# Tokens on partitions for the residual stream, and a Strassen down projection, in a two-layer decoder trunk

## The chip, the cores and the metric

One core of one Trainium2 chip. The metric is the device time of one execution in microseconds (us). Three runs of the kernel before gave 1452.82, 1452.92 and 1454.23; the median is 1452.92.

## The reference

Two pre-norm layers over 512 tokens of width 1024, all in float32:

```
for i in 0, 1:
    h = rms_norm(x, norm_mix[i])
    x = x + mixer_i(h)                      # 0: gated delta rule + differential attention; 1: forgetting attention
    h = rms_norm(x, norm_mlp[i])
    x = x + square(relu(h @ w_mlp_up[i])) @ w_mlp_down[i]          # 1024 -> 4096 -> 1024
    x = x + (p[i] @ w_ple_proj[i]) * sigmoid(x @ w_ple_gate[i])    # 256 -> 1024, 1024 -> 1024
out = rms_norm(x, norm_final)
```

Each mixer ends with a projection of its eight heads' outputs, `y = heads @ w_out` (1024 by 1024).

## The kernel before, in words

**Products.** Every large product is made exact to about float32 by splitting both operands in a high part (rounded to the fast format, by ScalarE) and a low part (the difference, by VectorE), and taking three matmuls a k tile of 128: high by high, low by high, high by low. A weight arrives by DMA on SyncE's queue in pieces of 512 KB (`wraw`, into one of three buffers `raw`), and `wsplit` makes the pair of it (one of three buffers `whl`, 8 KB a partition). `wload` does that for two pieces, 1024 rows by 256 columns. `gemm` makes one tile of 128 features by 512 tokens in 24 matmuls of 512 columns: the weight is the stationary operand, the activations move.

**The residual stream** lies with features on partitions: `x_all`, eight tiles of 128 features by 512 tokens. In layer 0 it is read anew in `out_proj`, 256 columns at a time, and turned by 32 transposes of 128 by 128. `norm_tile` weights and splits a feature tile at once; the factor of each token (`norm_sum`, `norm_spread`: eight matmuls of 2 columns and two of 512) is applied later, behind the next product. That is what lets the next product start before the norm's sum is known. `p_proj` (the product of the layer's input embedding) stands between `out_proj` and the MLP, and `norm_sum` is put in its middle. In layer 1 the first query and key projection of the mixer (`ahead`) plays that part.

**MLP.** The 4096 hidden features go in four groups g of 1024. `up_group(g)` makes eight tiles u (24 matmuls each; relu and factor on VectorE, the square on GpSimd, the split on ScalarE and VectorE). `down_group(g)` makes eight tiles of 24 matmuls and adds each to the stream (`add_x`). The order is up 0, up 1, down 0, up 2, down 1, up 3, down 2, down 3. A layer has 768 matmuls up and 768 down.

**Order of the work.** The program's text gives priorities; a scheduler at compile time orders each engine's instructions by them and by which operands its own timing of the program has ready. So a later product's matmuls can stand between the steps of an earlier chain on TensorE. Every engine runs its own list in order, waiting at semaphores; so does each queue that issues DMAs (SyncE's for weights, ScalarE's for small inputs).

**Rooms.** Tiles come from pools. The pools `cp`, `raw`, `whl` and `hl` (16 tiles of 4 KB, for the split activations) live through the whole program. The mixers' pools (`gp` in layer 0, `fp` in layer 1) are closed when the mixer's text ends, and the pools opened after that (`xp`, `lp`, `tp`, then `mp`, `qp`) take the same room. `p_split` loads p into `pr`, a tile of `tp`, by a DMA on ScalarE's queue.

**The last part** (`ple_last`) turns the stream to tokens on partitions by 32 transposes, and makes 16 tiles of 128 tokens by 256 features, 24 matmuls of 256 columns each.

Of the kernel before, what the change touches and what calls it, by code (L numbers as in the profile page):

```python
# [10 lines left out]
F32 = mybir.dt.float32  # L11
# [31 lines left out]
def constants():  # L43
    """Masks, the identity and the rotary frequencies: they depend on shapes alone."""
# [23 lines left out]
MM = 3  # banks of the projections' sums  # L68
LAT_A, LAT_B = 1.55, 1.7  # stretch the waits between the steps of a chain of delta rule, of attention
W_G, W_B, W_T, W_V, W_Q = 10.0, 22.5, 20.0, 6.0, 3.6  # waits for what a chain starts from  # L70
Z_B, DSTEP = 3, 3.47
ORDER = "a0 a1 w0 v0 v1 b0 b1 a2 a3 w2 b2 b3"
ABREAST = 2  # heads of the delta rule at once
N_SP = 10  # tiles of theirs
N_ST = 5  # short-lived ones
N_WARM = 15  # products that bring TensorE's clock up


class Tensor:
    """TensorE, and how much work it has been given (us)."""  # L80
# [4 lines left out]
    def matmul(self, out, lhsT, rhs, start, stop):  # L85
        self.time += math.prod(rhs.shape[1:]) * (1 if rhs.dtype == F32R else 4) / 2400
        return self.tc.nc.tensor.matmul(out, lhsT=lhsT, rhs=rhs, start=start, stop=stop)  # L87
# [7 lines left out]
def trunk(ctx: ExitStack, tc: tile.TileContext, I, cst, out):  # L95
# [43 lines left out]
    # ------------------------------------------------------------------ constants  # L139
# [12 lines left out]
    xT, shared = [], {}  # L152
    cols = cp.tile([P, R_ALL], F32, name="cols")
    rstd_c = cp.tile([P, NT], F32, name="rstd_c")
# [58 lines left out]
    def narrow_steps(ws, act, pool, tag, bufs):  # L213
        """Eight columns of a projection, tokens on partitions; ws has high and low parts side by side."""
# [17 lines left out]
    def rsqrt(dst, ss, w, scale, eps=EPS, big=None, V=V):  # L232
        """dst = (ss * scale + eps) ** -0.5; with big, 0 where the sum has left the range."""
# [11 lines left out]
    def norm_tile(k, nrm, wcol):  # L245
        """One feature tile of x: its weighted split, and its share of the mean square."""
        hi, lo = hl()
        w = cols[:, wcol + k:wcol + k + 1]
        S.activation(out=hi, in_=xT[k], func=AF.Copy, scale=w)  # L249
        V.scalar_tensor_tensor(out=lo, in0=xT[k], scalar=w, in1=hi.bitcast(F32), op0=ALU.mult, op1=ALU.subtract)  # L250
        nrm["act"].append((hi, lo))
        if k == 0:
            S.activation(out=nrm["s"], in_=xT[k], func=AF.Square)
        else:
            q = nrm["pool"].tile([P, T], F32, tag="sq", name="sq", bufs=2)
            S.activation(out=q, in_=xT[k], func=AF.Square)  # L256
            G.tensor_tensor(out=nrm["s"], in0=nrm["s"], in1=q, op=ALU.add)  # L257

    def norm_begin(pool):
        s = pool.tile([P, T], F32, tag="nrm_s", name="nrm_s", bufs=1)  # L260
        return {"s": s, "act": [], "pool": pool}

    def norm_sum(nrm):
        parts = [nrm["pool"].tile([P, T], F32R, tag="sq", name=n, bufs=2) for n in ("s_hi", "s_lo")]
        split(*parts, nrm["s"])
        ps = aux()
        for i in range(NT):
            for j, a in enumerate(parts):
                PE.matmul(ps[:, 2 * i:2 * i + 2], lhsT=a[:, i * P:(i + 1) * P], rhs=ones_r[:, 0:2], start=j == 0,
                          stop=j == 1)  # L270
        rsqrt(rstd_c, ps[:, 0:2 * NT].rearrange("p (i c) -> p i c", c=2)[:, :, 0], NT, 1.0 / D, big=BIG)
        r = [nrm["pool"].tile([P, NT], F32R, tag=f"r{j}", name="r", bufs=1) for j in range(2)]
        split(*r, rstd_c)
        nrm["diag"] = parts
        for t, a in zip(parts, r):
            V.tensor_tensor(out=v3(t), in0=mid(ident), in1=a.bitcast(F32).broadcast_to([P, NT, P]), op=ALU.mult)

    def norm_spread(nrm):
        pb = aux()
        for j, t in enumerate(nrm["diag"]):  # L280
            PE.matmul(pb, lhsT=ones_r, rhs=t, start=j == 0, stop=j == 1)
        S.activation(out=shared["rstd_b"], in_=pb, func=AF.Copy)
        return nrm["act"]

    def add_x(m, ps):
        V.tensor_tensor(out=xT[m], in0=ps, in1=xT[m], op=ALU.add)  # L286

    # ------------------------------------------------------------------ mixer of layer 0
    def even_mixer(act, first, wba):
        w_in = I["w_in_even"][0]  # L290
        with ExitStack() as es:
# [16 lines left out]
            # gates of the delta rule: b and a columns, tokens on partitions  # L308
# [8 lines left out]
            def gates():  # L317
# [32 lines left out]
                # decays within the blocks on the diagonal  # L350
# [13 lines left out]
            def conv_tile(ps, j, name):  # L364
                """causal convolution and silu of one tile of qkv_a"""
# [1033 lines left out]
```

## Time and profile before

| | |
|---|---|
| median of three runs | 1452.92 us (1452.82 to 1454.23) |
| span of the profiled execution | 1453.0 us; the page gives no other time of it, so its own time is taken as 1453.0 |
| TensorE busy | 1420.3 us, 98%, 7095 matmuls |
| VectorE, ScalarE, GpSimd busy | 793.7 us (55%), 622.7 us (43%), 195.4 us (13%) |
| DMA | 129.46 MB, mean 89 GB/s |
| granted clock of TensorE, mean | 0.990 |

The page counts a matmul as busy from its start to a modelled end, and matmuls overlap, so the cost of one is read from start to start of the next, in the timeline. Times in rows are us from the span's start. The stages, read from TensorE's timeline: mixer of layer 0 to about 315, its output projection to 356, `p_proj` to 368, the MLP and the gate product to 773, the mixer of layer 1 to 997, its output projection to 1034, `p_proj` to 1046, the MLP to 1396, the rest to 1453.

### The profile page before, as it was taken

Reading aid. Unit: us, or ns where it says so; the run is one execution under the profiler, and the core shown is the slowest. Engines: PE = TensorE matmul, PEld = TensorE weight load, DVE = VectorE, ACT = ScalarE, POOL = GpSimd, SP = SyncE. Lnnn points to the kernel's source line nnn. Section 1 sums busy time; section 2 is a strip of 40 time slices with the busy share of each in tenths; the row PEclk is TensorE's granted clock in tenths of the full one; section 3 lists DMA queues with packets and bytes.
Section 4 is the critical chain, followed back from the end, with each engine's and each line's share of the span. In section 5 each row is a group of like instructions: output and inputs, shape, how many; then the busy total and the mean of one; then the engine's idle time right before and its main releaser. Section 6 shows DMA issues by size and latency. Waiting matters only on the chain.

```text
span 1453.0 us, 18378 instructions
## 1 busy us (share of the span) xinstructions
PE 1420.3 (98%) x7095; PEld 1184.1 (81%) x7095; DVE 793.7 (55%) x1396; ACT 622.7 (43%) x1061; POOL 195.4 (13%) x243
## 2 busy tenths in 40 slices
PE   8989988999999999999999999999999999999997
PEld 6877776778888888888888888887888888888897
DVE  6836785754454353443466856756455445354445
ACT  6746775665332231222355544545433222132244
POOL 1350056012121020100022000001122001010000
PEclk9999997999999999999999999999999999999999
DMA  6251212124233233223235443642323323323321
GB/s 175 79 102 45 59 46 59 44 73 145 88 96 107 88 98 105 88 95 108 87 88 99 64 85 73 66 89 88 94 87 101 102 88 101 101 88 102 102 98 63
DMA packets 144555, 129.46 MB, mean 89 GB/s; under 512 B 8578, under 2 KB 141524, under 8 KB 144212
## 3 DMA queue, kind: packets, MB, share of 16 engines
q1 hardware_dynamic: 140080, 123.82, 31.3%
q10 hardware_dynamic: 4388, 4.47, 1.4%
q8 instruction: 56, 0.92, 0.3%
q14 instruction: 31, 0.25, 0.1%
HBM read 126.04 MB, written 2.23 MB: 88 GB/s over the span
## 4 chain that ended last, share of the span: by engine, by line
PE 89%; DVE 3%; POOL 3%; DMA 2%; ACT 2%; issue 1%; ACTq 0%; SPq 0%; POOLq 0%; DVEq 0%
PE mm L87 78%; PE ax L87 8%; PE ax L91 2%; DMA raw<-w_in_even 1%; POOL xc L415 1%; DMA lb<-lsc 1%; POOL xt L413 1%; POOL b L389 0%; DVE whl L133 0%; DMA xr<-x 0%; POOL x L502 0%; POOL ro L615 0%; DMA pr<-p 0%; ACT L377 0%; POOL rot L673 0%
## 5 line engine op out<-in xcount | busy, mean ns | idle before, releaser
L87 PE MATMUL mm<-hl,whl 128*128 128x512 f32 x4032 | 961.8, 394 | 2.2 <-DVE whl L133 1.4
L87 PEld LDWEIGHTS mm<-hl,whl 128*128 128x128 f32 x4032 | 752.6, 189 | 157.3 <-DVE whl L133 2.1
L133 DVE TENSOR_TENSOR whl<-raw,whl 128x1024 fp32r<-128x1024 f32 (+1 forms) x223 | 295.0, 1323 | 192.7 <-ACT whl L130 192.5
L130 ACT ACTIVATE whl<-raw 128x1024 fp32r<-128x1024 f32 (+1 forms) x224 | 237.3, 1060 | 338.0 <-PE mm L87 320.1
L87 PE MATMUL mm<-ul,whl 128*128 128x512 f32 x768 | 176.5, 391 | 0.0
L87 PEld LDWEIGHTS mm<-ul,whl 128*128 128x128 f32 x768 | 144.2, 188 | 31.6
L1134 POOL TENSOR_TENSOR u<-r 128x512 f32<-128x512 f32 x64 | 66.7, 1042 | 464.5 <-DVE r L1132 464.5
L286 DVE TENSOR_TENSOR x_all<-mm,x_all 128x512 f32<-128x512 f32 x80 | 55.2, 691 | 111.6 <-PE mm L87 109.4
L87 PE MATMUL mm<-whl,hl 128*128 128x256 f32 x864 | 107.4, 284 | 0.0
L87 PEld LDWEIGHTS mm<-whl,hl 128*128 128x128 f32 x864 | 105.1, 192 | 0.3
L1132 DVE SCALAR_TENSOR_TENSOR r<-mm,rstd_b 128x512 f32<-128x512 f32 x64 | 44.3, 692 | 81.5 <-PE mm L87 74.0
L257 POOL TENSOR_TENSOR nrm_s<-nrm_s,sq 128x512 f32<-128x512 f32 x21 | 29.7, 1412 | 409.4 <-ACT sq L256 409.4
L130 ACT ACTIVATE ul<-u 128x512 fp32r<-128x512 f32 x32 | 20.2, 632 | 93.6 <-POOL u L1134 93.6
L130 ACT ACTIVATE hl<-u 128x512 fp32r<-128x512 f32 x32 | 20.2, 633 | 87.7 <-POOL u L1134 87.7
L133 DVE TENSOR_TENSOR hl<-u,hl 128x512 fp32r<-128x512 f32 x32 | 21.9, 685 | 30.1 <-ACT hl L130 30.1
L133 DVE TENSOR_TENSOR ul<-u,ul 128x512 fp32r<-128x512 f32 x32 | 21.9, 685 | 30.1 <-ACT ul L130 30.1
L844 DVE TENSOR_TENSOR ax<-ax,cmask 128x128 f32<-128x128 f32 x64 | 18.7, 295 | 17.0 <-PE ax L87 16.6
L249 ACT ACTIVATE hl<-x_all,cols 128x512 fp32r<-128x512 f32 x24 | 17.3, 721 | 24.6 <-DVE x_all L286 17.9
L130 ACT ACTIVATE hl<-x_all 128x512 fp32r<-128x512 f32 x16 | 10.0, 625 | 40.2 <-DVE x_all L286 37.9
L250 DVE SCALAR_TENSOR_TENSOR hl<-x_all,cols,hl 128x512 fp32r<-128x512 f32 x24 | 18.0, 749 | 10.6 <-ACT hl L249 10.5
L669 ACT ACTIVATE rot<-mm 32x512 f32<-32x512 f32 x32 | 18.9, 589 | 9.6 <-DMA raw<-w_in_even 4.9
L87 PE MATMUL ax<-qk 128*128 128x256 f32 (+2 forms) x96 | 21.9, 335 | 0.1
(351 smaller groups left out, 1261.4 us busy)
## 6 DMA issues: line engine op xcount, KB each, us to landing
raw<-w_mlp_up SPq DMA_DIRECT2D x64, 512.0 KB, 3.7
raw<-w_mlp_down SPq DMA_DIRECT2D x64, 512.0 KB, 3.4
raw<-w_in_even SPq DMA_DIRECT2D x32, 256.0 KB, 3.5
raw<-w_ple_gate SPq DMA_DIRECT2D x16, 512.0 KB, 3.4
raw<-w_in_odd SPq DMA_DIRECT2D x32, 256.0 KB, 6.0
raw<-w_in_odd SPq DMA_DIRECT2D x16, 512.0 KB, 4.8
raw<-w_in_even SPq DMA_DIRECT2D x12, 512.0 KB, 3.8
raw<-w_out_even SPq DMA_DIRECT2D x8, 512.0 KB, 3.4
```

The lines of the kernel that those rows point to most:

```text
L87: return self.tc.nc.tensor.matmul(out, lhsT=lhsT, rhs=rhs, start=start, stop=stop)
L91: return self.tc.nc.tensor.transpose(out, in_, ident)
L130: S.activation(out=hi, in_=src, func=AF.Copy)
L133: return (E or V).tensor_tensor(out=lo, in0=src, in1=hi.bitcast(F32), op=ALU.subtract)
L249: S.activation(out=hi, in_=xT[k], func=AF.Copy, scale=w)
L250: V.scalar_tensor_tensor(out=lo, in0=xT[k], scalar=w, in1=hi.bitcast(F32), op0=ALU.mult, op1=ALU.subtract)
L257: G.tensor_tensor(out=nrm["s"], in0=nrm["s"], in1=q, op=ALU.add)
L286: V.tensor_tensor(out=xT[m], in0=ps, in1=xT[m], op=ALU.add)
L669: S.activation(out=rot[32 * b:32 * b + 32], in_=ps[32 * (b ^ 1):32 * (b ^ 1) + 32], func=AF.Copy)
L844: V.tensor_tensor(out=ps[:, c], in0=ps[:, c], in1=cmask, op=ALU.add)
L1132: V.scalar_tensor_tensor(out=r, in0=ps, scalar=0.0, in1=rstd_b, op0=ALU.max, op1=ALU.mult)
L1134: G.tensor_tensor(out=u, in0=r, in1=r, op=ALU.mult)
```

## The change

The stream lies with tokens on partitions, `x_tok`, four tiles of 128 tokens by 1024 features, loaded by four DMAs of 512 KB on SyncE's queue after the first mixer. All products that add to it now have the activations stationary (128 tokens) and 512 columns of weights moving. The norm is applied before the next product: `Norm.scaled` makes the scaled tile of 128 tokens and `features` turns it with eight transposes and splits it. That is done in both `out_proj`, behind both MLPs, and behind the first gate product. `p_split` and `p_proj` move behind the MLP. The first four pieces of an output projection's weight go to tiles `owhl` of a pool `op` that is opened after the mixer; of the other four, three go to `whl`.

The down projection of each group is done as seven products of half-size blocks (256 tokens, 512 of k, 512 features) in Strassen's scheme in Winograd's form, 24 matmuls of 512 columns each: 168 a group in place of 192. The sums of blocks are made by GpSimd, in float32, before the split: four sums of weight blocks (two instructions of 128 by 1024 each) and four of activation blocks (two of 128 by 512 each). The squares stay on GpSimd, the relu goes to ScalarE. For the first three groups each product is followed by one tile of the next up group.

The diff, cut to its core:

```diff
+SRAW, SWHL, SA = 8, 3, 4
+ORDER_MID, ORDER_END = (1, 5, 6, 7, 3, 4, 2), (1, 2, 5, 6, 3, 7, 4)
...
-    def norm_tile(k, nrm, wcol): ...
-    def norm_begin(pool): ...
-    def norm_sum(nrm): ...
-    def norm_spread(nrm): ...
+    def tok_steps(ps, act, w, i, cs, kts, first, last):
+        for j, kt in enumerate(kts):
+            ah, al = (a[:, i * P:(i + 1) * P] for a in act[kt])
+            PE.matmul(ps, lhsT=ah, rhs=w[:, 0, j, cs], start=first and j == 0, stop=False)
+            PE.matmul(ps, lhsT=ah, rhs=w[:, 1, j, cs], start=False, stop=False)
+            PE.matmul(ps, lhsT=al, rhs=w[:, 0, j, cs], start=False, stop=last and j == 1)
+
+    def features(i, src, act):
+        for c in range(2):
+            ps = aux2()
+            for b in range(4):
+                PE.transpose(ps[:, b * P:(b + 1) * P], src[:, (4 * c + b) * P:(4 * c + b + 1) * P], ident)
+            for b in range(4):
+                hi, lo = (a[:, i * P:(i + 1) * P] for a in act[4 * c + b])
+                split(hi, lo, ps[:, b * P:(b + 1) * P])
...
+        def scaled(self, i, src):
+            t, r, ok = small(1, "tn"), small(1, "rn"), small(1, "okn")
+            V.tensor_scalar(out=t, in0=self.ssq[:, i, 0:1], scalar1=self.ssq[:, i, 1:2], scalar2=EPS, ...)
+            V.tensor_scalar(out=ok, in0=t, scalar1=BIG / D, scalar2=None, op0=ALU.is_lt)
+            V.tensor_scalar(out=t, in0=t, scalar1=BIG / D, scalar2=None, op0=ALU.min)
+            G.tensor_tensor(out=r, in0=t, in1=nhalf[:, 0:1], op=ALU.pow)
+            V.tensor_tensor(out=r, in0=r, in1=ok, op=ALU.mult)
+            xn = ...
+            V.scalar_tensor_tensor(out=xn, in0=src, scalar=r, in1=self.wb, op0=ALU.mult, op1=ALU.mult)
+            return xn
...
+    def whole_weight(w, pool, pairs=range(4)):
+        op_bufs["owhl"] = 4
+        return [[wide(w, 2 * P * j, 512 * c, rawp, *((whp,) if c and n < 3 else (pool, "raw", "owhl")))
+                 for n, j in enumerate(pairs)] for c in range(2)]
+
+    def out_proj(w, heads, norm, pairs):
+        act = [hl() for _ in range(KT)]
+        with tc.tile_pool(name="op", bufs=1) as op:
+            first, second = whole_weight(w, op, pairs)
+            sums = [acc(), acc(), acc(), aux2()]
+            for n, j in enumerate(pairs):
+                for i in range(NT):
+                    tok_steps(sums[i], heads, first[n], i, slice(0, 512), (2 * j, 2 * j + 1), n == 0, n == 3)
+            for i in range(NT):
+                add_x(i, slice(0, 512), sums[i])
+                norm.squares(i, 0, x_tok[i][:, 0:512])
+            turned = []
+            for i in range(NT):
+                ps = acc()
+                for n, j in enumerate(pairs):
+                    tok_steps(ps, heads, second[n], i, slice(0, 512), (2 * j, 2 * j + 1), n == 0, n == 3)
+                add_x(i, slice(512, 1024), ps)
+                norm.squares(i, 1, x_tok[i][:, 512:1024])
+                turned.append(norm.scaled(i, x_tok[i]))
+                if i:
+                    features(i - 1, turned[i - 1], act)
+        return act, lambda: features(NT - 1, turned[NT - 1], act)
...
+    def down_products(w, g, us, mp, order):
...
+        def combine(out, a, b, op):
+            for o, p, q in zip(out, a, b):
+                G.tensor_tensor(out=o, in0=p, in1=q, op=op)
+            return out
+        def right(p):
...
+            if p == 5:
+                sums["T"] = combine(block(0, 0), block(0, 1), block(0, 0), ALU.subtract)
+            elif p == 6:
+                combine(sums["T"], block(1, 1), sums["T"], ALU.subtract)
+            elif p == 7:
+                return combine(block(0, 1), block(1, 1), block(0, 1), ALU.subtract)
+            elif p == 4:
+                combine(sums["T"], block(1, 0), sums["T"], ALU.subtract)
+            return sums["T"]
+        def left(p):
...
+        for p in order:
+            ws = [wide_split(t, mp, "swhl") for t in right(p)]
+            acts = []
+            for t in left(p):
+                a = mp.tile([P, 2, 2, 256], F32R, tag="sa", name="sa", bufs=SA)
+                split(a[:, 0], a[:, 1], t)
+                acts.append(a)
...
+            for j in range(2):
+                for t in range(2):
...
+            for t in range(2):
+                add_x(2 * th + t, slice(512 * fh, 512 * fh + 512), banks[name][t])
+            yield p
...
             for g in range(1, 4):
-                cur = up_group(g)
-                down_group(g - 1, prev)
+                cur = []
+                ups = up_steps(g, cur)
+                for _ in down_products(down, g - 1, prev, mp, ORDER_MID):
+                    next(ups)
+                for _ in ups:
+                    pass
                 prev = cur
-            down_group(3, prev)
+            xs = [hl() for _ in range(KT)]
+            for p in down_products(down, 3, prev, mp, ORDER_END):
+                if p == 7:
+                    for i in range(2):
+                        features(i, x_tok[i], xs)
+                    between()
+            for i in range(2, NT):
+                features(i, x_tok[i], xs)
...
+        pT = []
+        xs = mlp(layer, act, last_tile, lambda: pT.extend(p_split(layer)))
+        with tc.tile_pool(name=f"qp{layer}", bufs=1) as pool:
+            pj = [pool.tile([P, D], F32, name=f"pj{i}") for i in range(NT)]
+            p_proj(layer, pT, pj)
...
+            act = ple(layer, xs, pj, pool, norm)
```

In the first up tiles of a layer the two tiles are made in halves of 256 tokens, and the last token tile's `features` (`last_tile`) stands between the halves. The gate product of layer 1 has tiles of 512, 256 and 256 columns in place of four of 256.

## Rows read from the trace of the kernel before

**Rows 1.** The page, busy time of each engine over the span.
```profile
PE 1420.3 (98%) x7095; PEld 1184.1 (81%) x7095; DVE 793.7 (55%) x1396; ACT 622.7 (43%) x1061; POOL 195.4 (13%) x243
```

**Rows 2.** The page, chain that ended last, share of the span by engine.
```profile
PE 89%; DVE 3%; POOL 3%; DMA 2%; ACT 2%; issue 1%; ACTq 0%; SPq 0%; POOLq 0%; DVEq 0%
```

**Rows 3.** Timeline of TensorE, MLP: start us, us, engine, line, operation out<-moving,stationary, form, count.
```profile
586.56 87.25 PE L87 MATMUL mm<-hl,whl 128*128 128x512 f32 x384
673.65 44.13 PE L87 MATMUL mm<-ul,whl 128*128 128x512 f32 x192
```

**Rows 4.** The same view, embedding product of layer 1: weights move, activations stand.
```profile
1041.77 4.45 PE L87 MATMUL mm<-whl,pT 128*128 128x512 f32 x18
1046.06 5.63 PE L87 MATMUL mm<-hl,whl 128*128 128x512 f32 x24
```

**Rows 5.** The same view: four transposes and what follows; the norm's small matmuls, first and last.
```profile
337.84 0.60 PE L91 MATMUL ax<-gen,raw 128*128 128x128 f32 x4
338.20 5.75 PE L87 MATMUL mm<-hl,whl 128*128 128x512 f32 x24
...
362.97 0.17 PE L87 MATMUL ax<-ones,s_hi 128*128 128x2 f32 x1
...
363.78 4.38 PE L87 MATMUL mm<-pT,whl 128*128 128x512 f32 x18
```

**Rows 6.** The same view, last gate product, 256 columns.
```profile
1403.75 41.83 PE L87 MATMUL mm<-whl,hl 128*128 128x256 f32 x346
```

**Rows 7.** The same view, layer 0: output projection's matmuls between the last heads' steps, first and resumption.
```profile
299.59 2.34 PE L87 MATMUL mm<-hl,whl 128*128 128x512 f32 x9
...
315.10 3.93 PE L87 MATMUL mm<-hl,whl 128*128 128x512 f32 x16 [0.42 <-ACT hl L916]
```

**Rows 8.** The same in layer 1, first and the one behind the last head's matmuls.
```profile
980.98 1.10 PE L87 MATMUL mm<-hl,whl 128*128 128x512 f32 x4
...
996.93 6.05 PE L87 MATMUL mm<-hl,whl 128*128 128x512 f32 x25
```

**Rows 9.** Timeline of VectorE and ScalarE's queue where the mixers end, layer 0 and layer 1.
```profile
313.73 1.47 DVE L133 TENSOR_TENSOR hl<-zt,hl 128x512 fp32r<-128x512 f32 x2
315.23 0.40 ACTq L1167 DMA_DIRECT2D pr<-p  x1
...
998.53 0.69 DVE L133 TENSOR_TENSOR hl<-gate,hl 128x512 fp32r<-128x512 f32 x1 [0.70 <-ACT hl L130]
999.31 0.39 ACTq L1167 DMA_DIRECT2D pr<-p  x1
```

**Rows 10.** Windows: stretch, length, busy PE PEld DVE ACT POOL, granted clock, DMA share, GB/s.
```profile
108.00:112.00 4.00, 2.75 (x6) 1.79 (x7) 2.68 (x7) 3.23 (x6) 0.60 (x1) 0.66 0.47 133
112.00:116.00 4.00, 4.00 (x11) 2.79 (x9) 1.35 (x4) 1.75 (x3) 0.69 (x1) 0.50 0.02 6
```

**Rows 11.** Weight tile in the MLP of layer 0 (ns min/median/max, first and last start); one collision.
```profile
L130 ACT ACTIVATE whl<-raw x64: 1046/1062/1062, 377.1 to 717.9; 128x1024 fp32r<-128x1024 f32 x64
L133 DVE TENSOR_TENSOR whl<-raw,whl x64: 1224/1226/1866, 378.2 to 719.0; 128x1024 fp32r<-128x1024 f32 x64
...
423.95 1.04 POOL L1134 TENSOR_TENSOR u<-r 128x512 f32<-128x512 f32 x1 [4.40 <-DVE r L1132]
...
424.21 1.87 DVE L133 TENSOR_TENSOR whl<-raw,whl 128x1024 fp32r<-128x1024 f32 x1 [0.40 <-ACT whl L130]
```

**Rows 12.** Instructions by line and form: busy us, mean ns; the first from one tile's view.
```profile
L257 POOL TENSOR_TENSOR nrm_s<-nrm_s,sq x21: 1275/1292/1795, 326.4 to 1036.6; 128x512 f32<-128x512 f32 x21
...
L133 POOL TENSOR_TENSOR whl<-raw,whl 128x1024 fp32r<-128x1024 f32 x1 | 2.4, 2402 | 4.3 <-ACT whl L130 4.3
L242 POOL TENSOR_TENSOR rs_t<-rs_t,nhalf 128x4 f32<-128x4 f32 x7 | 7.1, 1012 | 60.7 <-DVE rs_t L241 60.7
L286 DVE TENSOR_TENSOR x_all<-mm,x_all 128x512 f32<-128x512 f32 x80 | 55.2, 691 | 111.6 <-PE mm L87 109.4 <-ACT x_all L1112 2.1
L133 DVE TENSOR_TENSOR ul<-u,ul 128x512 fp32r<-128x512 f32 x32 | 21.9, 685 | 30.1 <-ACT ul L130 30.1
```

More of the change, by code (lines that the diff above doesn't have):

```diff
@@ L259, in norm_begin @@
[L259 to L286, printed above, removed]
+    def wide(src, r0, c0, pool_raw, pool_w, raw_tag="raw", tag="whl"):
+        return wide_split(wide_raw(src, r0, c0, pool_raw, raw_tag), pool_w, tag)
@@ L1162, in mlp @@
-        return xs
-    def p_split(layer, pool):
-        pr = pool.tile([P, NT, 256], F32, name="pr")
+                    sums = [acc(), acc()] if g + c == 0 else []
+                    if g + c == 0:
+                        for half in range(2):
+                            hs = slice(256 * half, 256 * half + 256)
+                            for m in range(2):
+                                gemm(sums[m][:, hs], w, m, [(a[:, hs], b[:, hs]) for a, b in act])
+                            if half == 0:
+                                last_tile()
@@ new lines, in p_proj, with ple @@
+            for i in range(NT):
+                ps = acc()
+                tok_steps(ps, pT, w, i, slice(0, 512), (0, 1), True, True)
+                S.activation(out=pj[i][:, 512 * c:512 * c + 512], in_=ps, func=AF.Copy)
+    def ple(layer, xs, pj, pool, norm):
+        final = layer == 1
+        ot, rs = [], []
+        act = None if final else [hl() for _ in range(KT)]
+        w = whole_weight(I["w_ple_gate"][layer], pool)
+        spans = [(0, 512), (512, 256), (768, 256)] if final else [(0, 512), (512, 512)]
+        if final:
+            ot = [pool.tile([P, D], F32, name=f"ot{i}") for i in range(NT)]
+            part = pool.tile([P, NT], F32, name="part")
@@ L1277, in ple_last @@
-                hold(V.tensor_tensor(out=ot[:, i, cs], in0=xt[:, i, cs], in1=nf[:, cs], op=ALU.mult))
-                if c == 2:
-                    V.tensor_reduce(out=part[:, i:i + 1], in_=ssq[:, i, 0:3], axis=AX.X, op=ALU.add)
-                    V.tensor_scalar(out=part[:, i:i + 1], in0=part[:, i:i + 1], scalar1=EPS, scalar2=None, op0=ALU.add)
-                if c == D // 256 - 1:
+                hold(norm.squares(i, n, x_tok[i][:, cs]))
+                if not final:
+                    if last:
+                        turned.append(norm.scaled(i, x_tok[i]))
+                        if i:
+                            features(i - 1, turned[i - 1], act)
+                    continue
@@ L1282, in ple_last @@
+                hold(V.tensor_tensor(out=ot[i][:, cs], in0=x_tok[i][:, cs], in1=norm.wb[:, cs], op=ALU.mult))
+                if n == 1:
+                    V.tensor_scalar(out=part[:, i:i + 1], in0=norm.ssq[:, i, 0:1], scalar1=norm.ssq[:, i, 1:2],
+                                    scalar2=EPS, op0=ALU.add, op1=ALU.add)
+                if last:
                     if rs:
@@ L1351, in trunk @@
                         op0=ALU.mult)
+    xp = None
     for layer in range(2):
```

341 lines of the change are left out of this document (144 added, 197 removed).

## The prediction

> **What bounds the kernel now.** I read the busy times first: TensorE is busy 98% of the span, no other engine more than 55% [rows 1]. The chain that ended last says the same of the end: 89% of it is TensorE, and it names no second engine above 3% [rows 2]. So the time is TensorE's list, and a change is worth the matmuls that it takes off this list, less the idle time that it puts in. TensorE's timeline gives the price of a matmul, from start to start: in the MLP 384 of them take 673.65 - 586.56 = 87.09 us, 0.227 us each, without a hole [rows 3]. The profiled execution's span, 1453.0 us, is the base of the sum; the median of three runs is 1452.92, within 0.01%.
>
> **Matmuls, removed and added.** Down projection: 2 layers x 4 groups x 192 = 1536 matmuls at 0.227 go, 348.7 us. 2 x 4 x 168 = 1344 come. They move weights over stationary activations, and both lie in new rooms. The one place of before where 512 columns of weights move has 18 in 4.29 us, 0.238 each; activations moving cost 0.227 [rows 3, 4]. Since those 18 hold one change of bank, I take 0.232: 311.8 us, a gain of 36.9 (ends 43.6 and 28.8).
>
> Transposes: 64 go (x into layer 0, the stream out at the end), 160 come (five times 32 in `features`). Four and the step to the next matmul take 0.36 us, 0.09 each [rows 5]: +8.6. The norm's eight small matmuls (0.81 us) and two of 512 columns (2 x 0.227, an estimate from rows 3) go three times: -3.8 [rows 5]. The first up tiles of both layers are made in halves of 256 columns, 0.12 us each [rows 6]: 2 x (96 x 0.12 - 48 x 0.227) = +1.2. The last gate product has 96 wide and 192 narrow matmuls for 384 narrow: -0.8. The 576 others that now move weights (both output projections, the first gate product) cost 0.005 more each: +2.9. Sum of TensorE's list: -36.9 + 8.6 - 3.8 + 1.2 - 0.8 + 2.9 = **-28.8**. `p_split` and `p_proj` only move; their 48 matmuls and 16 transposes cost the same in the new place.
>
> **The two joints between mixer and output projection.** Before, the output projection's weights lie in `whl`, which lives all the time, so its matmuls fill TensorE while the last heads' chains finish: in layer 0 the first stands at 299.59 and 52 of them are done at 315.10; in layer 1, 36 stand between 980.98 and 996.93 (TensorE was put on other steps between them) [rows 7, 8]. After, the pieces needed first go to `owhl`, in a pool that takes the mixer's room. When is such a room free? The only tile of before that shows it is `pr`: its DMA is issued at 315.23 and 999.31, 0.03 and 0.09 us behind the end (313.73 + 1.47 and 998.53 + 0.69) of the last read of any tile of the mixer's pool (`zt`, `gate`) by VectorE [rows 9]. I read it as: a new pool waits for the whole old one. So the first high part starts at 315.2, is 1.06 us on ScalarE, and the low part 1.23 on VectorE [rows 11]: 317.5. Lost in layer 0: 52 x 0.227 = 11.8 and 317.5 - 315.1 = 2.4. In layer 1: 36 x 0.227 = 8.2, and 999.2 + 2.3 - 996.9 = 4.6. Together 27.0. Behind the waiting split on ScalarE stand only the squares and other splits of the same stage, and on SyncE's queue the four loads of `x_tok`, needed 96 matmuls (22 us) later: nothing more is late.
>
> The clock comes on top. With holes of this kind in layer 0's mixer (TensorE busy 2.75 of 4 us) the granted clock fell to 0.66 and then 0.50, that is to 1.2 GHz for most of eight us; the pulses lost are 0.34 x 4 + 0.50 x 4 = 3.4 us [rows 10]. TensorE will now have two sparser stretches of 16 to 18 us, each followed by dense work. I take 2.5 for each, two thirds of it: 5.0. The joints cost **+32.0** (ends: 20, if the chains end 3.5 us sooner for being alone and the clock holds; 34).
>
> **The three joints at a norm.** Behind the last token tile's product stand, one after another: the add 0.69, the square 0.8, three tiny steps 0.5, the power on GpSimd 1.0, the factor 0.2, the scaling 1.2 (as a low part of 1024), transposes 0.4, the first split 0.6: 5.4 us (the add and the power from [rows 12], the scaling from [rows 11], the others estimates from their sizes against these). Cover: before each up group, 48 narrow matmuls (5.8 us); before the second mixer, the value projection of three token tiles (72 narrow ones, 8.6 us). So the chain itself just fits. What is late next is VectorE: in the same 11 us it has three tiles' adds, scalings, 24 splits of 128 columns and the next two weight pieces. I take 2.3 us a joint, **+7** (ends 0 and 15).
>
> **GpSimd against VectorE in the MLP.** In the MLP a weight's low part takes 1.224 to 1.226 us, or up to 1.866 when GpSimd's square runs: that one began at 424.21, the square ended at 424.99, and 1.09 us behind that the low part ended [rows 11]. GpSimd too is held: 1.292 becomes 1.795 [rows 12]. So the two take turns. Before, GpSimd had one square of 1.04 a tile. Count now one group, in us. GpSimd: 8 squares of 1.04, 8 sums of 128 by 512 at 1.29, 8 of 128 by 1024 at 2.40 (its one low part of that size) [rows 11, 12]: 8.3 + 10.3 + 19.2 = 37.8. VectorE's low parts: 14 of a block at 1.225, 14 of an activation at 0.685, 8 of an up weight: 17.2 + 9.6 + 9.8 = 36.6. The sum, 74.4, has to fit in one line beside TensorE's 192 x 0.227 + 168 x 0.232 = 82.6. That goes, with little slack: through products 5, 6 and 7 it needs 13.4 per step of 11 us. I take 1 us of idle time for each of the six interleaved groups (ends 0 and 5).
>
> The last group of a layer has nothing between its products: 39.0 us of TensorE against 17.2 + 9.6 + 10.3 + 19.2 = 56.3 in that line. The buffers let 16.0 of it be done ahead (the block sums of products 5 and 7, three `swhl`, four `sa`), so 40.3 remain. VectorE also has 14 adds at 0.69 and 16 features' low parts, about 0.28 each (an estimate from 0.685 for four times the columns, and the fixed part): 14.2. Were all of these beside GpSimd's turns, the line would take 40.3; were none, 54.5. The trace has no such add beside a GpSimd instruction. The Trainium skill, page "SBUF — State Buffer", section "Who interferes with whom", says that only an instruction of VectorE with two operands in SBUF contends with GpSimd's reads; adds and features read one from PSUM, so by it the group would end 1.3 us late, not 8. I take the middle, 47.4, since each engine runs its list in order: 8 us late, twice. Together **+22** (ends 0 and 61).
>
> What I cost at nothing: the relu on ScalarE (37 us of work a group beside 82.6); the hand-over of the MLP's room to the next weights, which `p_proj`'s 48 matmuls (11 us) hide, up to 5 us if they didn't; the broadcast loads of norm weights on ScalarE's queue, needed 25 us later; the wider rows of the weight DMAs.
>
> **Sum.** 1453.0 - 28.8 + 32.0 + 7 + 22 = **1485**.
>
> **Rivals.** (1) Ready weights, not slower: the first pieces of the output projections are split before the mixers end, so the fill stays. Place: 299.6 to 317.5 and 981 to 1001.5; price -32: 1453. It decides as soon as the first `owhl` stands before 315 and 998. Against it: `pr` waited in both layers; for it: that is one tile on another queue. (2) Hidden helpers: buffers and the reach of 1.5 products cover GpSimd's turns and the norms' chains; -29: 1456. For it: the mean load fits in every interleaved group. With (1) also true it is 1424, and only then is the change plainly faster. (3) The turns bind: each interleaved group loses 5 and each last one 15.5, +39: 1524. For it: 13.4 against 11 in three steps, and sums made in place wait for the splits that read them. That the product count wouldn't fall isn't a rival: 7 for 8 is written out.
>
> **How the numbers follow.** Chances: forecast 0.48, (1) alone 0.10, (2) alone 0.16, both 0.13, (3) 0.13. The forecast's own range, by the ends of the joints and a few us on the matmul price, is 1462 to 1508. The range to hold 8 in 10 goes down past 1453 and 1456 to 1440, and up to 1520, just short of (3). 0.2% (3 us) is about what a measurement tells from no change. Faster: both (0.13) and shares of (1) and (2) alone, 0.21. Same: 0.07. Slower: 0.72.
>
> **What would show it.** Right: about 18 us from 299.6 in which TensorE has only single steps of heads, and the same near 981; a granted clock of 0.5 there; `owhl` first written behind the last low part of a mixer; low parts of 1024 columns of 1.2 us alone and over 2 beside a block sum of 2.4; the fourth group of each layer 45 us or more for 168 matmuls; the interleaved groups near 83. Wrong: output projection matmuls among the last heads' steps, a fourth group of 39 us, or a matmul of the new kind outside 0.227 to 0.238.

## The result, and the profile after

The kernel after takes 1489.26 us (median of 4 runs, 1488.77 to 1492.47), the kernel before 1452.93 in the same runs: ratio 1.0254, 95% interval 1.024 to 1.0269. That is 36 us more; the forecast was 1485, 32 more. The profiled execution of after has a span of 1490.7 us, 37.7 over that of before, and a mean granted clock of 0.968 in place of 0.990. It is the longest of the four executions of after, so a difference read from its trace can come out up to 3 us larger than that of the medians.

The page of after, busy times, and the chain that ended last by engine, answer to [rows 1, 2]:

```profile
PE 1411.6 (95%) x6969; PEld 1170.4 (79%) x6969; DVE 989.6 (66%) x1591; ACT 720.3 (48%) x1326; POOL 499.4 (33%) x359
...
PE 25%; DVE 2%; issue 1%; ACT 0%; POOLq 0%; DVEq 0%; ACTq 0%
```

TensorE has 126 matmuls fewer, and its busy share fell from 98% to 95%. GpSimd works 2.6 times as long, and is still idle two thirds of the time. The chain is no help here: its shares add to 28%, since it was not followed back further.

Windows of after, by stage (columns as in [rows 10]). From above: end of the first mixer, first norm joint, an interleaved group, the last group with what follows it, the norm joint before the second mixer, end of the second mixer.

```profile
299.90:310.09 10.19, 2.89 (x13) 1.85 (x13) 6.79 (x16) 5.61 (x14) 2.33 (x3) 0.63 0.05 9
...
360.11:368.24 8.13, 2.24 (x12) 1.60 (x10) 5.01 (x20) 4.76 (x17) 0.55 (x1) 0.73 0.10 20
...
416.93:498.53 81.60, 81.60 (x362) 67.59 (x361) 58.59 (x50) 34.96 (x44) 44.98 (x22) 1.00 0.34 104
...
661.90:713.47 51.57, 46.44 (x205) 37.20 (x204) 45.90 (x56) 23.51 (x43) 24.05 (x12) 0.93 0.07 21
...
772.65:781.55 8.90, 1.98 (x9) 1.57 (x9) 5.62 (x20) 4.50 (x15) 3.98 (x9) 0.74 0.06 8
...
1009.00:1023.05 14.05, 5.96 (x24) 4.52 (x22) 5.71 (x15) 4.55 (x9) 0.00 (x0) 0.74 0.03 7
```

The interleaved group is full: 360 matmuls in 81.60 us, 0.2267 each, TensorE busy all the time at the full clock, although VectorE and GpSimd are busy for 58.6 + 45.0 us beside it. The others have holes, and a granted clock under 1.

*The joint of mixer and output projection*, layer 0 (answers to [rows 7]), timeline of TensorE; then the engines that release it there and in layer 1 (answers to [rows 9]).

```profile
298.79 1.18 PE L89 MATMUL mm<-hl,whl 128*128 128x512 f32 x4
301.08 0.63 PE L93 MATMUL ax<-gen,u 128*128 128x128 f32 x4 [1.12 <-DVE u L638]
303.64 1.11 PE L93 MATMUL ax<-gen,u 128*128 128x128 f32 x4 [1.93 <-DVE u L638]
306.69 1.09 PE L93 MATMUL ax<-gen,do 128*128 128x128 f32 x4 [1.94 <-DVE do L931]
310.09 7.42 PE L89 MATMUL mm<-owhl,hl 128*128 128x512 f32 x18 [2.31 <-ACT owhl L132]
317.35 1.56 PE L89 MATMUL ax<-owhl,hl 128*128 128x512 f32 x6
```

```profile
307.06 1.47 DVE L135 TENSOR_TENSOR hl<-zt,hl 128x512 fp32r<-128x512 f32 x2
...
308.98 2.95 ACT L132 ACTIVATE owhl<-raw 128x1024 fp32r<-128x1024 f32 x3 [0.48 <-DVE hl L135]
...
1020.78 0.69 DVE L135 TENSOR_TENSOR hl<-gate,hl 128x512 fp32r<-128x512 f32 x1 [0.69 <-ACT hl L132]
...
1021.94 2.95 ACT L132 ACTIVATE owhl<-raw 128x1024 fp32r<-128x1024 f32 x3 [1.19 <-DVE hl L135]
```

`owhl` is begun 0.45 and 0.47 us behind the end of the last read of a tile of the mixer's pool (307.06 + 1.47 and 1020.78 + 0.69), and until then TensorE has only the heads' steps. In layer 0 that stretch, from 299.97 to 310.09, is 10 us long; I had forecast about 18. The six matmuls from 317.35 take 1.40 us, to 318.75: with weights from `owhl` one costs 0.2333, at the full clock.

*The norm joint*, layer 0, timeline of SyncE's queue, then of TensorE, VectorE and ScalarE together.

```profile
329.26 37.23 SPq L168 DMA_DIRECT2D raw<-w_mlp_up  x3
```

```profile
353.75 4.36 PE L89 MATMUL mm<-whl,hl 128*128 128x512 f32 x18
...
359.35 1.03 PE L93 MATMUL ax<-gen,xn 128*128 128x128 f32 x8
...
362.80 1.28 DVE L304 SCALAR_TENSOR_TENSOR raw<-x_tok,rn,wb 128x1024 f32<-128x1024 f32 x1
...
364.13 1.97 PE L93 MATMUL ax<-gen,raw 128*128 128x128 f32 x8 [3.75 <-DVE raw L304]
...
365.28 0.28 ACT L132 ACTIVATE hl<-ax 128x128 fp32r<-128x128 f32 x1 [0.50 <-PE ax L93]
...
366.76 0.48 ACT L132 ACTIVATE hl<-ax 128x128 fp32r<-128x128 f32 x2 [0.19 <-DVE hl L135]
367.14 1.05 ACT L132 ACTIVATE whl<-raw 128x1024 fp32r<-128x1024 f32 x1
...
368.24 0.80 PE L89 MATMUL mm<-hl,whl 128*128 128x256 f32 x2 [2.14 <-ACT whl L132]
...
369.50 2.72 PE L89 MATMUL mm<-hl,whl 128*128 128x256 f32 x11 [0.46 <-DVE whl L135]
```

The 48 narrow matmuls that need only the first token tiles were to stand in this hole. They stand behind it: TensorE's list has the last tile's transposes (364.13) first, and the first up weight, asked for at 329.26, is split at 367.14, behind five of the last tile's eight high parts (the first is the one at 365.28) in ScalarE's list, with no wait of its own in front. Its rooms in `whl` were there too: the last matmuls that read them are the 18 from 353.75.

*The last group*, layer 0, where GpSimd's sums and VectorE's low parts meet; and the forms by busy time (answers to [rows 11, 12]).

```profile
672.09 2.83 POOL L1146 TENSOR_TENSOR sraw<-sraw 128x1024 f32<-128x1024 f32 x1
...
672.60 3.40 DVE L135 TENSOR_TENSOR swhl<-sraw,swhl 128x1024 fp32r<-128x1024 f32 x1
...
674.88 2.25 POOL L1146 TENSOR_TENSOR sn<-sn,u 128x512 f32<-128x512 f32 x1
...
675.92 1.27 DVE L308 TENSOR_TENSOR x_tok<-ax,x_tok 128x512 f32<-128x512 f32 x2
676.65 8.95 PE L89 MATMUL ax<-swhl,sa 128*128 128x512 f32 x31 [2.35 <-DVE x_tok L308]
```

```profile
L1146 POOL TENSOR_TENSOR sraw<-sraw 128x1024 f32<-128x1024 f32 x64 | 190.5, 2980 | 38.5 <-DVE swhl L135 37.4 <-issue 0.2
...
L135 DVE TENSOR_TENSOR swhl<-sraw,swhl 128x1024 fp32r<-128x1024 f32 x112 | 202.3, 1806 | 74.4 <-ACT swhl L132 74.0
```

A low part of 1.2 us lasts 3.40 beside a sum: it ends 1.08 behind the sum's end. The next sum (674.88) then lasts 2.25 in place of 1.29. The two adds behind the low part wait for it in VectorE's list, and TensorE waits 2.35 us for the adds.

**The ledger.** Idle time of TensorE over 0.3 us, added up, rose from 23.2 to 68.5 us; pulses that the clock withheld (length times one minus the granted clock, added up over the span) from 14.8 to 48.1 us, part of them in idle time. Against that stands the shorter list. The experiments put a price on each.

### The profile page after: what moved, and what is told of

Its sections match the earlier page's. It is cut to its first block, busy times and chain, and to the rows that moved or that the text cites. A ratio compares the mean times of both kernels' runs of the same rounds, so it can differ in the third digit from the quotient of the medians.

```text
span 1490.7 us, 18636 instructions
## 1 busy us (share of the span) xinstructions
PE 1411.6 (95%) x6969; PEld 1170.4 (79%) x6969; DVE 989.6 (66%) x1591; ACT 720.3 (48%) x1326; POOL 499.4 (33%) x359
## 5 line engine op out<-in xcount | busy, mean ns | idle before, releaser
L89 PE MATMUL mm<-hl,whl 128*128 128x512 f32 (+1 forms) x2784 | 661.7, 390 | 8.1 <-ACT whl L132 4.3
L89 PEld LDWEIGHTS mm<-hl,whl 128*128 128x128 f32 x2784 | 509.5, 192 | 109.4 <-DVE whl L135 6.2
L89 PE MATMUL ax<-swhl,sa 128*128 128x512 f32 x1344 | 321.5, 396 | 10.2 <-DVE swhl L135 5.5
L89 PEld LDWEIGHTS ax<-swhl,sa 128*128 128x128 f32 x1344 | 255.8, 191 | 67.2 <-DVE swhl L135 7.2
L135 DVE TENSOR_TENSOR whl<-raw,whl 128x1024 fp32r<-128x1024 f32 x139 | 214.9, 1551 | 111.4 <-ACT whl L132 110.8
L135 DVE TENSOR_TENSOR swhl<-sraw,swhl 128x1024 fp32r<-128x1024 f32 x112 | 202.3, 1806 | 74.4 <-ACT swhl L132 74.0
L1146 POOL TENSOR_TENSOR sraw<-sraw 128x1024 f32<-128x1024 f32 x64 | 190.5, 2980 | 38.5 <-DVE swhl L135 37.4
L132 ACT ACTIVATE swhl<-sraw 128x1024 fp32r<-128x1024 f32 x112 | 118.5, 1058 | 119.2 <-PE ax L89 96.4
L89 PE MATMUL mm<-whl,hl 128*128 128x256 f32 (+2 forms) x1032 | 168.0, 320 | 2.0 <-ACT whl L132 1.8
L89 PE MATMUL mm<-owhl,hl 128*128 128x512 f32 (+1 forms) x456 | 111.5, 397 | 6.1 <-ACT owhl L132 6.0
L1229 ACT ACTIVATE r<-mm 128x512 f32<-128x512 f32 x64 | 38.1, 595 | 133.5 <-PE mm L89 133.5
L135 DVE TENSOR_TENSOR sa<-u,sa 128x512 fp32r<-128x512 f32 x64 | 62.3, 973 | 10.4 <-ACT sa L132 10.4
```

Source lines behind the costliest of these rows:

```text
L132: S.activation(out=hi, in_=src, func=AF.Copy)
L135: return (E or V).tensor_tensor(out=lo, in0=src, in1=hi.bitcast(F32), op=ALU.subtract)
L1146: G.tensor_tensor(out=o, in0=p, in1=q, op=op)
L1229: S.activation(out=r, in_=ps, func=AF.Relu)
```

## The experiments

Differences are of medians, to 1489.3 (the kernel after) if nothing else is said. Line numbers differ a little between the kernels.

**1. Weights that are ready before the mixer ends.** In both output projections:

```diff
-    *((whp,) if c and n < 3 else (pool, "raw", "owhl"))
+    *((whp,) if n < 3 else (pool, "raw", "owhl"))
```

> The kernel after (1489.3 us) with three of the first four pieces of each output projection's weight in `whl` instead of `owhl`, so that they can be split before the mixer's room is free. Theory (the pool's hand-over takes the fill away): output projection matmuls stand between the last heads' steps again; by the trace after, the two joints lost about 11 us in layer 0 (52 matmuls x 0.227 = 11.8, 3.2 back since the bare chain ends sooner, 2.7 of half clock behind it) and 15 in layer 1, so about -27: 1462 us. Rival (the fill only slows the heads' chains, and the weights of the mixer's end need the same three rooms): within 5 us of 1489.

Measured 1465.97 us (1463.84 to 1466.73), **-23.3**; 1.0088 of before (1.0071 to 1.0105). Its timeline at the end of the first mixer:

```profile
305.89 1.88 PE L89 MATMUL mm<-whl,hl 128*128 128x512 f32 x7
308.07 0.66 PE L93 MATMUL ax<-gen,u 128*128 128x128 f32 x4 [0.29 <-DVE u L638]
308.48 1.64 PE L89 MATMUL mm<-whl,hl 128*128 128x512 f32 x6
311.12 0.63 PE L93 MATMUL ax<-gen,do 128*128 128x128 f32 x4 [1.00 <-DVE do L931]
```

The fill is back, and the clock stays at 1.00 from 302 to 314 (0.63 above). The hand-over of the room is the cause; its price, 23, is under the 27 that I had expected from the trace.

**2. The same work in the order that the cover needs**, at the three norm joints, with two rooms of `whl` left free for the next product's weight:

```diff
-    *((whp,) if c and n < 3 else (pool, "raw", "owhl"))
+    *((whp,) if c and n < 1 else (pool, "raw", "owhl"))
...
+    def behind(marks, work):            # queue work's instructions behind these, each on its engine
+        with ExitStack() as es:
+            for ins in marks:
+                es.enter_context(tc.issue_after(ins.ins))
+            work()
...
-                if i:
-                    features(i - 1, turned[i - 1], act)
+                if i == 1:
+                    features(0, turned[0], act)
+                    w, marks = load(), tuple(latest)      # next product's first weight and its two splits
+                elif i:
+                    behind(marks, lambda: features(i - 1, turned[i - 1], act))
...
-                                last_tile()
+                                behind((PE.last,), last_tile)
```

> The kernel after with the order changed at the three norm joints and no work added or taken: the weight of the next product (first up weight of each layer, value weight of the second mixer) is split before the token tiles are turned, two rooms of `whl` being left free for it, and the last token tile's transposes stand behind the matmuls that need only the first tiles. Theory (the cover that was there in the text was not there in ScalarE's and TensorE's lists): the three joints, 10.9, 10.9 and 10.4 us of idle time and half clock in the trace after, fall to about 2 each: -25, 1464 us. Rival A (VectorE's chain of add, factor and scaling with 24 small splits sets it whatever the order): about 4 us of the idle time stay in each joint, -12, 1477. Rival B (the half clock there comes from earlier, not from the hole): -15.

Measured 1469.77 us (1466.21 to 1473.52), **-19.5**. TensorE at the first joint, and three rows on what took the holes' place (first up group; gate product of layer 0):

```profile
362.83 1.03 PE L94 MATMUL ax<-gen,xn 128*128 128x128 f32 x8
363.62 5.99 PE L89 MATMUL mm<-hl,whl 128*128 128x256 f32 x48
369.45 1.03 PE L94 MATMUL ax<-gen,raw 128*128 128x128 f32 x8
370.42 0.97 PE L89 MATMUL mm<-hl,whl 128*128 128x256 f32 x5
```

```profile
391.89 5.38 DVE L136 TENSOR_TENSOR whl<-raw,whl 128x1024 fp32r<-128x1024 f32 x2
...
394.00 2.33 PE L89 MATMUL mm<-hl,whl 128*128 128x512 f32 x9 [2.33 <-DVE whl L136]
```

```profile
747.76 1.09 ACT L133 ACTIVATE whl<-raw 128x1056 fp32r<-128x1056 f32 x1 [4.96 <-DMA raw<-w_in_odd]
```

Of the hole at the first joint 1.07 us are left, of that at the second nothing, which refutes rival A: VectorE's chain fits under the narrow matmuls. This run changes two things, order and rooms. In the trace of after the rooms had been read for the last time before the hole began, so there it was the order that held the split; what the order alone would give, without the two rooms, was not run. New waits stand against the gain, 8.3 us in all. Two low parts of up weights take 5.38 us beside GpSimd's sums (2.33 idle, in both layers). Before the second mixer ScalarE's list now stands 4.96 us at a weight that has not landed, ahead of the squares on the path (3.69 idle).

**3. Half clock without the waiting.** 16 matmuls that nobody reads in the first hole of the two norm joints at an MLP:

```diff
+        ps = acc()
+        for _ in range(16):
+            tc.keep_in_program_order(PE.matmul(ps, lhsT=ones_r, rhs=heads[0][0], start=True, stop=True))
         return act, lambda: features(NT - 1, turned[NT - 1], act)
```

> The kernel after with 16 matmuls of 512 columns more in each layer, whose results nobody reads, on TensorE between the third token tile's transposes and the last one's, where the trace after has 3.75 us of idle time (the second hole, 2.14 us behind the transposes, stays). It tells half clock from waiting. Theory (the clock falls because of the hole, and the matmuls behind it pay): the granted clock stays at 1.00 from the joint on, the matmuls and transposes that took 3.8 us longer in each joint do not: -7.6, 1481.7 us. Rival A (the second hole alone is enough, or the halved clock goes with the narrow matmuls): 1489, within 2. Rival B (the added matmuls are late and stand in the way): +1 to +4.

Measured 1489.91 us (1489.76 to 1491.22), **no gain**: my theory missed, and the time is rival A's. Windows of this run (granted clock of after in the same stretches: 0.50, 0.50 and 0.73), then two rows of its TensorE:

```profile
364.00:368.00 4.00, 2.06 (x13) 1.29 (x12) 2.69 (x9) 2.33 (x8) 0.00 (x0) 1.00 0.13 24
368.00:372.00 4.00, 3.24 (x18) 3.04 (x19) 4.00 (x7) 3.47 (x7) 0.00 (x0) 0.78 0.96 332
372.00:376.00 4.00, 4.00 (x29) 4.00 (x28) 1.49 (x2) 0.27 (x1) 0.00 (x0) 0.79 0.96 284
```

```profile
360.18 1.03 PE L93 MATMUL ax<-gen,xn 128*128 128x128 f32 x8
...
368.00 0.50 PE L89 MATMUL mm<-hl,whl 128*128 128x256 f32 x2 [1.94 <-ACT whl L132]
```

The clock was held through the first hole, and it bought little there, because what follows waits for the split of the weight anyway. This execution reaches the joint 0.83 us later than that of after (360.18 and 359.35); counted from there the first up matmul comes 7.8 us behind in place of 8.9, and the first Strassen product 57.0 in place of 57.6 (layer 1: 55.9 in place of 57.6). Behind the second hole the clock falls all the same, for a shorter time. The pulses withheld in the whole span fell from 48 to 38.5 and the time did not, so the pulses counted in the ledger are not a price; the waits are, and run 2 takes those away.

**4. Last groups without block sums**, as eight plain products, each added to the stream:

```diff
-            for p in down_products(down, 3, prev, mp, ORDER_END):
+            for p in plain_products(down, 3, prev, mp):      # for kh, fh, th: 24 matmuls, two add_x
```

> The kernel after with the last group of each layer done as eight plain block products (192 matmuls, no block sums) in place of seven. Theory (in the last group the sums on GpSimd and the low parts on VectorE take turns, and TensorE waits 5.1 us and runs 4 us longer at half clock): without sums the group has neither, 24 matmuls x 0.227 = 5.4 come, 9.1 go: -3.7 a layer, 1482 us. Rival (the holes are those of a short product chain, its splits and its adds, and stay without sums): +5.4 a layer, 1500 us.

Measured 1485.24 us (1484.16 to 1486.0), **-4.0**: 192 matmuls are faster here than 168. The group lasts 47.81 us in both layers (51.57 and 51.45 in after), so in the traces the two groups give 7.4. This execution's first mixer ended 2.6 us later than that of after (its last transposes at 309.30 and 306.69), on the same instructions, and after's profile is its longest execution, so the medians show less. The first 168 matmuls have no hole:

```profile
663.15:701.24 38.09, 38.09 (x170) 31.49 (x169) 16.99 (x22) 8.21 (x10) 1.04 (x1) 1.00 0.05 14
```

VectorE's work fell too (it splits 16 blocks in place of 28), so this alone doesn't say which of the two it was. The next run does.

**5. The same seven products, the sums on VectorE:**

```diff
-                G.tensor_tensor(out=o, in0=p, in1=q, op=op)
+                (E or G).tensor_tensor(out=o, in0=p, in1=q, op=op)      # E is VectorE in the fourth group
```

> The kernel after with the block sums of the last group of each layer on VectorE in place of GpSimd; seven products as before. It tells taking turns from a mere lack of VectorE's time. Theory (turns: the sums occupy VectorE's time wherever they run, and at GpSimd's slower rate, 2.4 against 1.2 for a weight and 1.29 against 0.69 for an activation): the common line gets shorter by about 14 us a group, some of it ahead of the group; the last groups lose 2 to 5 us in place of 9: -8 to -14, about 1478 us. Rival (two engines side by side; VectorE's own list sets the group): VectorE gets 15 us more in each, +6 to +12 a layer, 1500 us or more.

Measured 1483.24 us (1482.8 to 1486.61), **-6.0**, less than I expected but on the side of the turns. The 144 matmuls up to the last product, this run and then after:

```profile
663.41:698.36 34.95, 34.57 (x157) 28.20 (x156) 32.23 (x44) 19.21 (x27) 1.04 (x1) 1.00 0.10 31
```

```profile
661.90:703.85 41.95, 36.82 (x145) 29.03 (x144) 38.18 (x34) 18.21 (x23) 24.05 (x12) 0.92 0.04 13
```

VectorE got the sums as well and is busy for a shorter time, 32.23 in place of 38.18: what it lost in after was waiting inside its own low parts. The group gains 7 us there and gives part of it back in two holes of 1.39 and 1.22 us behind, where the splits of p and of the turned tiles stand in line after the sums. Runs 4 and 5 both also take away the wait for a sum that is slow on GpSimd (2.98 us for a weight in after). Together they show that GpSimd's sums make the loss; that they make it by holding VectorE is read from the rows at 672.09 to 676.65 and from the busy times here.

**6. Plain products in all groups**: the number of products alone, where nothing else changes.

```diff
-                for _ in down_products(down, g - 1, prev, mp, ORDER_MID):
+                for _ in plain_products(down, g - 1, prev, mp):
```

> All groups done as eight plain block products, each followed by one up tile; no sums at all. Theory (the interleaved groups lose nothing to the turns, so the count of matmuls decides): six groups x 24 x 0.2267 = +32.6 against the run with only the last groups plain: 1482 + 32.6 = 1515 us. Rival (interleaved groups hide a loss of some us each behind modelled ends): under +25, below 1507 us.

Measured 1511.71 us (1510.69 to 1514.58), +26.5 on run 4. The three interleaved groups of layer 0, this run, then run 4:

```profile
413.24:674.36 261.12, 261.12 (x1153) 216.22 (x1152) 104.38 (x120) 77.78 (x96) 24.96 (x24) 1.00 0.30 91
```

```profile
418.16:663.15 244.99, 244.99 (x1081) 202.61 (x1080) 176.19 (x151) 105.11 (x133) 127.60 (x64) 1.00 0.34 104
```

16.13 us a layer for 72 matmuls, 0.224 each, both without a hole: the turns cost an interleaved group nothing. The rest to 32.6 is elsewhere: the first up group is 1.5 us shorter a layer without sums beside it, and in the profiled executions the first mixer ended 3 us sooner here (306.19 and 309.30), which has nothing to do with the edit.

**7. All together.** Edits 1, 2 and 4, the value weight asked for one token tile later, and the first group's sums held behind the fifth square. The second half of an output projection's weight now lies wholly in `owhl`.

> The kernel after with all three edits together: first pieces of the output projections in `whl` (1466.0 alone, -23.3), the next product's weight split early and the last token tile behind the first tiles' matmuls (1469.8 alone, -19.5), plain block products in the last groups (1485.2 alone, -4.0); and two waits mended that the second of them showed: the value weight of the second mixer is asked for one token tile later (3.7 us idle in the gate product), and the block sums of the first group are queued behind the fifth square on GpSimd (2.3 us idle in each layer's first up tiles). If the terms add: 1442.5, less up to 10 for the mended waits: 1432 to 1443 us, 10 to 20 under the kernel before (1452.9). Rival (they share one cost, the clock behind the holes): 1448 to 1456, no better than before.

Measured 1443.12 us (1442.42 to 1445.55): 0.9931 of before (0.9918 to 0.9944). The three gains add to 46.8 and the run has 46.1, so the edits don't share a cost. My two mends did nothing: 2.57 us idle in each first up group, 3.75 in the gate product.

**8. The mends, once more**: sums behind the eighth square, two rooms more for `owhl` in layer 0's gate product, where the value weight is asked for as in run 2 again; and the same with the sums of edit 5 in place of the plain last groups.

> The run with all edits (1443.1 us) with its two left-over waits mended another way: the first group's block sums stand behind all eight of its squares on GpSimd (in that run they stood ahead of the last ones, and two low parts of up weights beside them took 6.7 us in place of 2.5, 2.6 us of idle time and some half clock in each layer); in the gate product of layer 0 two rooms more for the weight's second half, so that the next weight's transfers start sooner (there ScalarE's list stood 5.1 us at a weight that had not landed, 3.75 us idle). If both go: -3 each layer and -4: 1433 us. Rival (the sums are then late for the second product): the idle time moves to the end of the first up group, 1441 to 1444.

> As the other run of this pair, but the last groups keep seven products, with the block sums on VectorE (alone -6.0) in place of eight plain products (alone -4.0). By those two: 2 us less than the other run, about 1431. Rival (what they gave apart was half clock, which is gone here, so that the 24 matmuls saved show in full, 5.4 a layer less 2.6 of idle time): 5 us less.

Measured 1454.9 (1453.91 to 1459.13) and 1455.86 (1450.31 to 1457.45): **12 us worse**. The gate product's hole went, but the sums were now late for the second, third and fourth product: 1.25, 3.04, 2.41 and 2.82 us of idle time in the first interleaved group of layer 0, the like in layer 1. I had named that rival, and priced it at the 2.6 it would save. Between them the two ways of doing the last group show no difference, where I had expected 2 to 5 us.

**9. One sum behind each square**, from the second on, and the rooms of run 8:

```diff
+            for o, p, q in zip(out, a, b):
+                mark = next(marks, None) if not g and o.shape[-1] == 512 else None
+                with tc.issue_after(mark.ins) if mark else nullcontext():
+                    G.tensor_tensor(out=o, in0=p, in1=q, op=op)
```

> The run with all edits (1443.1 us), with the two rooms more in the gate product of layer 0 (there the 3.75 us hole went, in the run of 1454.9), and the first group's block sums spread, one behind each square from the second on, in place of five in a row behind the fifth (2.6 us idle in each layer) or all behind the eighth (9.7 us idle in each layer). Theory (a sum beside the splits costs them its own 2.4 us, so it is the crowding that makes TensorE wait): no idle time over 1 us in the first up tiles nor in the first interleaved group; -4 and -2.6 to -3.5 a layer: 1433 us. Rival (in any order the sums of this group cost about 2.5 us): 1439.

Measured **1428.7 us** (1426.84 to 1429.81): 0.9823 of before (0.981 to 0.9837), 25 us faster. Against run 7 that is -14.4, where I had expected about -10; of the difference of the two traces 8.2 us are idle time and 5.9 pulses of the clock. The stretch with the first interleaved group, in the first run of 8 and here; then the page's busy line of this run:

```profile
403.00:440.00 37.00, 28.10 (x113) 21.34 (x111) 24.69 (x16) 14.56 (x19) 36.48 (x18) 0.95 0.08 26
```

```profile
403.00:440.00 37.00, 37.00 (x165) 30.61 (x164) 31.68 (x27) 17.37 (x23) 23.74 (x12) 1.00 0.31 100
```

```profile
PE 1394.2 (98%) x7017; PEld 1161.3 (81%) x7017; DVE 930.3 (65%) x1571; ACT 701.6 (49%) x1304; POOL 418.5 (29%) x327
```

Idle time over 0.2 us is 23.9 us (23.8 before the change) and the mean clock 0.990, as before the change. So what is left of the difference of spans, 1427.5 - 1453.0 = -25.5, is the list of matmuls.

## Why the prediction came near, and where its steps failed

The mechanisms were largely right, but that the sum came within 4 us was luck: errors of both signs met in it. The terms as shown, -36 + 23 + 32 + 18 = +37, make up the measured +36. Term by term, predicted against shown:

- **TensorE's list, -28.8: it was about -36.** In the Strassen products a matmul that moves weights takes 0.2267, not 0.232: 192 fewer are -43.5. The price of what goes was misread too: the matmuls that read `ul` in [rows 3], half of the down projection, take 0.229 (43.96 us for 192), 1.7 more to gain. Of the 576 others the 360 from `owhl` take 0.2333 and those from `whl` 0.228 to 0.233: some 3 more, as predicted. The transposes were nearly right: eight take 0.79 us (346.57 to 347.36), +9.5 for 96. The rest as predicted. Run 9 confirms it: -25.5 with 48 plain matmuls (10.9) put back, that is -36.4.
- **Mixer joints, +32: 23** (run 1). The mechanism and the place are as predicted, down to the half clock: the 18 matmuls from 310.09 take 7.26 us, 3.2 more than at 0.2267. Two sizes were off, and the term stayed inside the ends named. The heads' chain alone ended 6.7 us sooner (its last transposes at 306.69, before at 313.35), and not 3.5. That is one execution's figure: the profiles of runs 2 to 6, whose first mixers are the same, have these transposes between 306.19 and 309.68. And the first matmul needs only the high part, 1.6 us behind the room's release, not 2.3.
- **Norm joints, +7 (ends 0 and 15): about 32.** This is the term that was mis-sized, outside its ends. From the trace of after: holes of 7.1 and 6.8 us before the up groups and some 3.8 us at half clock in each, 10.4 for both before the second mixer. Run 2 bears it out: -19.5 with 8.3 of new waits. The chain was estimated a little short: from the last product, 359.35, to the end of the last tile's first high part, 365.56, are 6.2 us, and 6.5 to its first low part, for the 5.4 that I had; its transposes ran at half clock. What failed was the cover: "before each up group, 48 narrow matmuls". They were there in the text, but the weight that they need was behind the last tile in ScalarE's list, and the last tile ahead of them in TensorE's. Run 2, which changes the order and leaves two rooms free for that weight, takes the hole away. And I named VectorE as what is late next; it was not, but for the first up group's low parts beside the sums.
- **Turns of GpSimd and VectorE, +22: 18, in other places.** The six interleaved groups lost nothing (I had 6); run 6 shows it. The two last groups lost 9 each (I had 8): 51.57 us, less 168 x 0.2267 = 38.1 and 40 transposes, 4.2. Runs 4 and 5 show the cause. That the size came out at 8 was in part luck: it was the middle of two ends, as if half of VectorE's other work had no place beside GpSimd's turns. The two adds of 675.92 had one: they take 0.64 each beside a sum. The Trainium skill, page "SBUF — State Buffer", section "Who interferes with whom", says that a VectorE instruction with at most one input in SBUF does not contend with GpSimd, outside the two-port modes, and that one with two contends with a GpSimd instruction that reads SBUF. The rows agree with it, 0.64 for an add and 3.40 for a low part beside a sum. I had read from it a group only 1.3 us late. That did not follow: the adds are not held by GpSimd, but they stand in VectorE's list behind a low part that is. That each engine runs its list in order, the reason I gave, is what the rows show.

Of the rivals, ready weights alone (1453) was run 1's edit: the price of the joints in it was 9 too high. Hidden helpers was half right, for the interleaved groups. That the turns bind everywhere was wrong. The signs I named were seen: no fill in either joint, half clock in it, `owhl` behind the last low part, low parts over 2 us beside sums, a last group over 45. The interleaved groups came at 81.6 to 81.7, not near 83.

Open: why the compile-time order puts the first up weight's split so late, though on the chip its rooms and its data were there before the hole. No run tells it. Open too: why a matmul costs 0.2333 with weights from `owhl` and 0.2267 with those of the Strassen products, in the same form.

## What to carry to other kernels

A cover counts only if the lists have it: look in each engine's own order for the instruction that feeds the covering work, above all on the engine that splits or copies operands, before costing a chain as hidden. Opening a pool where an old one must close is a barrier for what is put in it, so put the first operands of the next product in a room that lives on. And where two engines take turns, spread the helper's work in single instructions between the other's: five sums in a row left TensorE idle for 2.6 us a layer, the same sums too late for 9.5, and one behind each square not at all.

## What was not expected of the hardware

- 512 columns cost 0.2267 us in the interleaved groups, whether weights or activations move, but 0.2333 with weights from `owhl`, so the direction does not set the price. The 0.238 of [rows 4] is 0.233 without its one longest step (0.315).
- VectorE and GpSimd together were busy for 104 us of work and waiting in a group of 81.6 us, and TensorE lost nothing by it.
- A held clock is not time won: 16 useless matmuls kept it at 1.00 in the hole, and the whole time stayed where it was (1489.9 and 1489.3).
